# Projecting the values by rows of tokens, stored to memory and loaded in two token orders, in a hybrid decoder layer

## The chip, the cores and the metric

The kernel runs on one core of one Trainium2 chip. The metric is the device time of one execution in microseconds (us). A core has five engines with instruction queues of their own: PE (matrix products; PEld is its weight load, which overlaps with products), DVE, ACT and POOL (elementwise work), and SP, which here issues the DMA transfers between memory (DRAM) and the on-chip buffer. Products land in PSUM, eight banks of 128 x 512 fp32.

## The reference

One decoder layer on 1024 tokens of width 1024, in fp32. The mixer has a pooling branch (256 channels) and twelve rotary attention heads of width 64, each evaluated three times, with keys at stride 1, 4 and 16. The change concerns the values v.

```python
h = rms_norm(x, ln_pre_mix[l])
proj = h @ w_in[l]
u_pool = proj[..., :POOL_WIDTH]
q = proj[..., POOL_WIDTH:POOL_WIDTH + ATTN_WIDTH].reshape(B, S, N_HEADS, HEAD_DIM)
k = proj[..., POOL_WIDTH + ATTN_WIDTH:POOL_WIDTH + 2 * ATTN_WIDTH].reshape(B, S, N_HEADS, HEAD_DIM)
v = proj[..., POOL_WIDTH + 2 * ATTN_WIDTH:].reshape(B, S, N_HEADS, HEAD_DIM)
q, k = rope(q, pos), rope(k, pos)
pool_out = multi_scale_pool(u_pool, w_pool[l], pool_scale[l])
attn_out = dilated_attention(q, k, v).reshape(B, S, ATTN_WIDTH)
mix = jnp.concatenate([pool_out, attn_out], axis=-1) @ w_out[l]
x = x + rms_norm(mix, ln_post_mix[l])
h = rms_norm(x, ln_pre_ffn[l])
f = (jax.nn.silu(h @ w_gate[l]) * (h @ w_up[l])) @ w_down[l]
x = x + rms_norm(f, ln_post_ffn[l])
```

## The kernel before

**Numbers.** Every fp32 operand of a product is split into a high and a low part of a faster type: ACT casts the high part (L151 for weights), DVE or POOL subtracts it for the low part (L155). A product is three matmuls, high-high, high-low and low-high. `wtile` loads a weight tile of 512 KB into one of two raw buffers (`wraw`) and splits it into one of two split buffers (`whl`).

**Attention.** The heads make six pairs and the tokens two halves: twelve units, pairs 0 to 3 one after the other with both halves, then pair 4 half 0, pair 5 half 0, pair 4 half 1, pair 5 half 1 (`pa` and `pb` are pairs 4 and 5). A unit has scores (`ps_s`, L114), exponentials on ACT (L535), a merge and weighing of the three evaluations (`weigh`, on POOL L586 and DVE), transposes of the weights (`ps_t<-pmt,pp` and `ps_t<-idt,pp`, L117; split into `ptr` by ACT L626 and DVE L627), and products with the values (`ps_o<-ptr,v`). Its result goes to memory (`mixd`) and comes back for the output projection (`mraw`, `m`, L863 to L869).

**Order.** PE's instructions keep the order in which the program emits them. A table of positions, counted in units (`PRM`, put into a plan and sorted), sets that order. Beside the steps of units it holds `Fill` objects: projections cut into single steps, drawn in threes at even distances through a unit, and one at a time by `pull` between matmuls whose operand is strided. The other engines' instructions are put in order by a scheduler, as buffers come free; each engine runs its own list strictly in order. Buffers come from named pools: PSUM tags pj, s, o and t have two banks each.

**Values.** `v_half` is a `proj_half` for one pair: weights stationary, 512 tokens moving, 24 matmuls into one pj bank; `v_done` (L447) scales by the token norm on DVE into `vT`, channels by tokens. `v_turn` then turns `vT` by PE transposes into the two token orders that the products want: `nat` 1, tokens with stride 4, each transpose preceded by a pulled fill matmul, and `nat` 0, contiguous. Four transposes fill a ps_t bank; ACT (L480) casts it and DVE (L481) subtracts. That is 288 matmuls and 96 transposes in all. Unit 0's fill is pair 0's values up to position 0.33, then the pooling projection (`pool_proj`, `ps_pj<-whl,x`, two token tiles of 256 columns in a bank, evicted by ACT at L697). The fills of the units 2, 4, 6, 7, 8, 9 and 10 hold the other values.

## Time and profile before

| | |
|---|---|
| runs (three) | 1203.65, 1204.16, 1205.82 us, median 1204.16 |
| profiled execution | 1204.66 us, span 1202.8 us, mean granted clock of PE 0.982 |
| attention | until about 490 us of the span |
| most executed PE group in it | 720 matmuls of 512 columns, `ps_pj<-x,whl`, 215.3 us busy |

The profile is read from the top: the share that each engine is busy, the chain of work that ended last, then single groups of instructions, with their busy time, mean duration in ns, and the idle time ahead of them with its releaser. Matmuls overlap, so a matmul of 419 ns mean duration does not take 419 ns of PE's stream; start times of neighbours give the pitch. A row of the timeline has start, length, engine, line, operation, names, and in brackets the idle time ahead and what ended it.

Two more rows help to place the transposes of values, 96 in PE's list, and what follows them.

```profile
L117 PE MATMUL ps_t<-idt,vT 128*128 128x128 f32 x96 | 20.0, 280 | 4.4 <-DVE ptr L627 4.0 <-DVE v L481 0.3
L117 PE MATMUL ps_t<-pmt,pp 128*128 128x128 f32 x180 | 28.7, 281 | 4.0 <-DVE v L481 3.9
```

### The profile page before, as it was taken

Reading aid. Unit: us, or ns where it says so; the run is one execution under the profiler, and the core shown is the slowest. Engines: PE = TensorE matmul, PEld = TensorE weight load, DVE = VectorE, ACT = ScalarE, POOL = GpSimd, SP = SyncE. Lnnn points to the kernel's source line nnn. Section 1 sums busy time; section 2 is a strip of 40 time slices with the busy share of each in tenths; the row PEclk is TensorE's granted clock in tenths of the full one; section 3 lists DMA queues with packets and bytes.
Section 4 is the critical chain, followed back from the end, with each engine's and each line's share of the span. In section 5 each row is a group of like instructions: output and inputs, shape, how many; then the busy total and the mean of one; then the engine's idle time right before and its main releaser. Section 6 shows DMA issues by size and latency. Waiting matters only on the chain.

```text
span 1202.8 us, 16715 instructions
## 1 busy us (share of the span) xinstructions
PE 1156.9 (96%) x5942; PEld 982.1 (82%) x5942; DVE 793.6 (66%) x1467; ACT 541.1 (45%) x1021; POOL 595.6 (50%) x537
## 2 busy tenths in 40 slices
PE   8999999999999799999999999999999999999996
PEld 6898988878888687878888888888888888888896
DVE  7947877676778656678865756566665465454585
ACT  7456655554546565475522232232322335443430
POOL 0141625354245222242276776577764977656521
PEclk9999999999999899989999999999999999999998
DMA  7111101011011312562044444455434759765642
GB/s 271 56 40 36 45 27 45 27 45 45 27 44 46 95 71 88 199 238 97 18 149 184 157 170 154 167 195 190 147 129 173 277 183 391 240 210 193 193 140 71
DMA packets 68435, 158.60 MB, mean 132 GB/s; under 512 B 8064, under 2 KB 11392, under 8 KB 66944
## 3 DMA queue, kind: packets, MB, share of 16 engines
q1 hardware_dynamic: 67776, 157.01, 37.2%
q8 instruction: 47, 0.77, 0.3%
q10 hardware_dynamic: 576, 0.52, 0.1%
q14 instruction: 36, 0.29, 0.1%
HBM read 114.51 MB, written 42.99 MB: 131 GB/s over the span
## 4 chain that ended last, share of the span: by engine, by line
PE 81%; DVE 10%; issue 3%; ACT 3%; DMA 2%; POOL 1%; SPq 0%; DVEq 0%; ACTq 0%; POOLq 0%
PE ps_pj L114 29%; PE ps_o L114 22%; PE ps_s L114 20%; PE ps_t L114 7%; PE ps_t L117 3%; DVE pp L532 1%; DVE whl L155 1%; DVE ptr L627 1%; DMA wraw<-in_w_out_dram 1%; DVE sq L999 1%; DMA mraw<-mixd 1%; DMA xraw<-in_xT_dram 0%; DVE k L340 0%; DVE rsw L315 0%; DVE v L481 0%
## 5 line engine op out<-in xcount | busy, mean ns | idle before, releaser
L114 PE MATMUL ps_pj<-x,whl 128*128 128x512 f32 x720 | 215.3, 419 | 1.5 <-ACT whl L151 0.9
L114 PEld LDWEIGHTS ps_pj<-x,whl 128*128 128x128 f32 x720 | 131.0, 192 | 19.0 <-ACT whl L151 1.1
L1218 POOL TENSOR_TENSOR fw<-rw,fw 128x512 fp32r<-128x512 f32 x74 | 101.8, 1401 | 65.4 <-ACT fw L1216 65.4
L586 POOL TENSOR_SCALAR pp<-pp,wv 128x256 f32<-128x256 f32 (+1 forms) x156 | 72.6, 485 | 106.2 <-DVE wv L570 100.2
L114 PE MATMUL ps_o<-tT,fw 128*128 128x512 f32 x504 | 117.8, 390 | 0.0
L535 ACT ACTIVATE pp<-pp,sx 128x128 f32<-128x128 f32 (+1 forms) x192 | 89.5, 468 | 48.2 <-DVE sx L532 47.7
L114 PEld LDWEIGHTS ps_o<-tT,fw 128*128 128x128 f32 x504 | 94.7, 188 | 20.0
L1218 POOL TENSOR_TENSOR whl<-rw,whl 128x512 fp32r<-128x512 f32 x42 | 63.4, 1533 | 59.5 <-ACT whl L1216 59.5
L1216 ACT ACTIVATE fw<-rw 128x1024 fp32r<-128x1024 f32 x37 | 38.5, 1057 | 97.6 <-DMA rw<-in_w_up_dram 29.4
L1360 POOL TENSOR_TENSOR op<-rw,op 128x512 fp32r<-128x512 f32 x38 | 60.0, 1580 | 38.2 <-ACT op L1359 37.6
L317 POOL TENSOR_TENSOR rsw<-rsw,sinr 128x512 f32<-128x512 f32 x20 | 26.2, 1308 | 105.3 <-DVE rsw L315 105.3
L1359 ACT ACTIVATE op<-rw 128x1024 fp32r<-128x1024 f32 x38 | 40.3, 1061 | 67.2 <-PE ps_t L114 26.7
L626 ACT ACTIVATE ptr<-ps_t 128x512 fp32r<-128x512 f32 (+1 forms) x84 | 48.3, 576 | 47.9 <-PE ps_t L117 43.1
L627 DVE TENSOR_TENSOR ptr<-ps_t,ptr 128x512 fp32r<-128x512 f32 (+1 forms) x84 | 55.9, 668 | 17.2 <-ACT ptr L626 16.3
L114 PE MATMUL ps_o<-ptr,v 128*128 128x128 f32 (+1 forms) x472 | 59.5, 262 | 4.6 <-DVE ptr L627 4.4
L155 POOL TENSOR_TENSOR whl<-wraw,whl 128x512 fp32r<-128x512 f32 x34 | 45.9, 1371 | 34.6 <-ACT whl L151 33.8
L114 PE MATMUL ps_pj<-b,fw 128*128 128x512 f32 x264 | 62.3, 392 | 0.0
L114 PEld LDWEIGHTS ps_o<-ptr,v 128*128 128x128 f32 x472 | 53.4, 168 | 8.3 <-DVE ptr L627 4.8
L114 PEld LDWEIGHTS ps_pj<-b,fw 128*128 128x128 f32 x264 | 49.6, 188 | 10.9
L114 PE MATMUL ps_s<-k,qh 128*128 128x128 f32 (+1 forms) x192 | 53.1, 287 | 3.4 <-DVE sx L532 3.4
L114 PEld LDWEIGHTS ps_s<-k,qh 128*128 128x128 f32 x192 | 48.3, 252 | 7.4 <-DVE sx L532 3.7
L114 PE MATMUL ps_o<-tT,whl 128*128 128x512 f32 x216 | 52.3, 397 | 0.0
(303 smaller groups left out, 2888.9 us busy)
## 6 DMA issues: line engine op xcount, KB each, us to landing
rw<-bd SPq DMA_DIRECT2D x77, 256.0 KB, 4.6
rw<-wsd SPq DMA_DIRECT2D x44, 256.0 KB, 4.0
rw<-in_w_gate_dram SPq DMA_DIRECT2D x20, 512.0 KB, 3.5
rw<-in_w_up_dram SPq DMA_DIRECT2D x20, 512.0 KB, 4.6
wraw<-in_w_in_dram SPq DMA_DIRECT2D x17, 512.0 KB, 3.5
bd<-p SPq DMA_DIRECT2D x33, 256.0 KB, 2.5
rw<-in_w_down_dram SPq DMA_DIRECT2D x33, 256.0 KB, 5.0
fw<-in_w_down_dram SPq DMA_DIRECT2D x16, 512.0 KB, 4.1
```

The source lines that it names most:

```text
L114: return tc.keep_in_program_order(nc.tensor.matmul(*a, **k))
L117: return tc.keep_in_program_order(nc.tensor.transpose(dst, src, by))
L155: eng.tensor_tensor(dst[:, 1, at:at + w], src[:, at:at + w], dst[:, 0, at:at + w].bitcast(F32), ALU.subtract)
L317: eng[0].tensor_tensor(s, s, sinr[:, sl], ALU.mult)
L535: nc.scalar.activation(pt[:, j, lo:], pt[:, j, lo:], AF.Exp, bias=sx[:, 0, side, j, hd, 0:1], scale=-1.0, accum_out=sx[:, 0, side, j, hd, ...
L586: nc.gpsimd.tensor_scalar(pv, pv, un.wv[:, side, j, hd:hd + 1], 1.0, op0=ALU.mult, op1=ALU.mult)
L626: nc.scalar.activation(ptr[:, 0, :w], t[:, :w], AF.Copy)
L627: nc.vector.tensor_tensor(ptr[:, 1, :w], t[:, :w], ptr[:, 0, :w].bitcast(F32), ALU.subtract)
L1216: nc.scalar.activation(w[n][:, :, 0], raw[n], AF.Copy)
L1218: low[0] = nc.gpsimd.tensor_tensor(w[n][:, i, 1], raw[n][:, i], w[n][:, i, 0].bitcast(F32), ALU.subtract)
L1359: nc.scalar.activation(w[:, :, 0], raw, AF.Copy)
L1360: nc.gpsimd.tensor_tensor(w[:, 0, 1], raw[:, 0], w[:, 0, 0].bitcast(F32), ALU.subtract)
```

## The change

Values of two pairs (256 columns of the weights) are projected at once, with 128 tokens stationary and the weights moving, so that they come out with tokens in the partitions. The weights are laid out anew on the host as a further input, `w_v`, in two tiles per two pairs (the two halves of the summed dimension, `kh`). `v_rows(n, h)` does half h of the tokens for pairs 2n and 2n + 1: 96 matmuls of 256 columns, in steps of two, over two pj banks of two token tiles each; the order is first half of the sum for both banks, then second half for both. ACT evicts a tile with the token norm as scale into `vs` (one buffer, shared with the rotary product of k), and SP stores two tiles to the DRAM tensor `vd`. `v_load` loads a half of a pair in both token orders into `vr` (one buffer), ACT casts and POOL subtracts. In all 576 matmuls of 256 columns, 12 stores and 24 loads of 256 KB, no transposes of values. Each call of `v_rows` but the two of unit 0 loads its own two weight tiles, ten in all where there were six. Unit 0 now projects the values of pairs 0 and 1, up to position 0.5; units 2, 4, 6 and 9 the rest; unit 10 has no fill left.

```diff
-        'vt': ((1.12, 1.16, 1.3, 1.58), (3.0, 3.1, 3.3, 3.58), (5.0, 5.1, 5.3, 5.58), (7.0, 7.1, 7.3, 7.58),
-               (8.95, 9.05, 9.2, 9.45), (10.08, 10.16, 10.36, 10.46)),
-        'pw': 0.33,
+        'vt': ((0.9, 1.06, 1.1, 1.16, 1.3, 1.45), (2.8, 3.0, 3.05, 3.1, 3.3, 3.45), (4.8, 5.0, 5.05, 5.1, 5.3, 5.45),
+               (6.8, 7.0, 7.05, 7.1, 7.3, 7.45), (8.8, 8.95, 9.0, 9.8, 9.88, 9.95), (9.98, 10.08, 10.12, 10.2, 10.36, 10.42)),
+        'pw': 0.5,
...
+    vd = dram.tile([NPAIR // 2, T, 2 * P], F32, name="vd")
...
-    def v_done(pr, h, ps):
...
-    def v_half(pr, h):
-        return proj_half(3 * pr.p + 2, h, pr.st, lambda ps: v_done(pr, h, ps))
...
+    def v_rows(n, h, box=None):
+        box = {} if box is None else box
+        def product(t, kh, k, i):
+            if (kh, k, i) == (0, 0, 0) and t % 2 == 0:
+                if "w" not in box:
+                    box["w"] = [wv0 if n + kk == 0 else wtile(w_v[n][kk]) for kk in range(2)]
+                box["ps", t // 2] = bank("pj")
+            ps = box["ps", t // 2][:, t % 2 * 256:t % 2 * 256 + 256]
+            a, b = PASSES[i]
+            at = h * 512 + t * P
+            mm(ps, xk[4 * kh + k][:, b, at:at + P], box["w"][kh][:, a, k * 256:k * 256 + 256],
+               start=(kh + k + i + t % 2 == 0), stop=(kh == 1 and k == 3 and i == 2), skip_group_check=True)
+            if (kh, k, i) == (1, 3, 2):
+                if t % 2 == 0:
+                    box["to"] = qkp.tile([P, 2, 256], F32, name="vs", tag="rcl", bufs=1)
+                nc.scalar.activation(box["to"][:, t % 2], ps, AF.Copy, scale=norm["r"][:, 4 * h + t:4 * h + t + 1])
+                if t % 2:
+                    did(("vd", n, h))
+                    nc.sync.dma_start(vd[n, at - P:at + P].rearrange("(j p) f -> p j f", p=P), box["to"])
+        jobs = [(t, kh, k, i) for t2, kh in ((0, 0), (2, 0), (0, 1), (2, 1)) for t in (t2, t2 + 1)
+                for k in range(4) for i in range(3)]
...
+        return [lambda x=jobs[i:i + 2]: two(x) for i in range(0, len(jobs), 2)]
...
-        def step(nat, h):
+        def load(h):
+            need(("vd", pr.p // 2, h), 2)
+            box[h] = qkp.tile([P, 2, 4, P], F32, name="vr", tag="vT", bufs=1)
+            src = vd[pr.p // 2, h * 512:h * 512 + 512, pr.p % 2 * P:pr.p % 2 * P + P]
+            nc.sync.dma_start(box[h][:, 1], src.rearrange("(r c) f -> r c f", c=4))
+            nc.sync.dma_start(box[h][:, 0], src.rearrange("(j r) f -> r j f", j=4))
+        def cut(nat, h):
             dst = pr.v[nat, h] = room(nat, h)
...
-            for j in range(4):
-                if nat:
-                    pull()
...
-                turned_to(t[:, j * P:(j + 1) * P], src, idt)
...
-            nc.scalar.activation(hi, tv, AF.Copy)
-            nc.vector.tensor_tensor(dst[:, :, :, 1], tv, hi.bitcast(F32), ALU.subtract)
...
+            nc.scalar.activation(hi, raw, AF.Copy)
+            nc.gpsimd.tensor_tensor(dst[:, :, :, 1], raw, hi.bitcast(F32), ALU.subtract)
...
-        fill[2 * p] += [q_half(pr, 1), v_half(pr, 0), v_half(pr, 1)]
+        fill[2 * p] += [q_half(pr, 1), v_rows(*((1, 0), (1, 1), (2, 0))[p - 1])]
...
-    fill[7] += [q_half(pa, 0), k_half(pa, 1), v_half(pa, 0)]
-    fill[8] += [v_half(pa, 1), k_half(pb, 0), q_half(pb, 0), k_half(pb, 1)]
-    fill[9] += [q_half(pa, 1), q_half(pb, 1), v_half(pb, 0)]
-    fill[10] += [v_half(pb, 1)]
+    fill[7] += [q_half(pa, 0), k_half(pa, 1), k_half(pb, 0)]
+    fill[8] += [q_half(pb, 0), k_half(pb, 1), q_half(pa, 1)]
+    fill[9] += [v_rows(2, 1), q_half(pb, 1)]
...
```

The positions of pool weights, pooling means and of unit 0's scores move by a few hundredths, and the flags that choose DVE for a split (`we`) are renumbered; two splits of value weights move from DVE to POOL. Row lines of the changed kernel are its own: L153 and L157 are the old L151 and L155, L319 and L322 the old L317 and L320, L603 the old L586, L886 the old L869.

Three places in the order follow; the numbers in names tell buffers apart. First PE in unit 0, where the values' projection comes to its second half of the sum. Before (the first value weights, in a buffer of k, `k_279`, stationary, 512 tokens moving, into one bank):

```order
L114 MATMUL ps_pj_353<-x6_119,k_279 128x512 x3
L117 MATMUL ps_o_398<-idt_265,n1r_376 128x128 x4
L114 MATMUL ps_pj_353<-x7_120,k_279 128x512 x3
L114 MATMUL ps_pj_422<-x0_113,k_279 128x512 x3
L117 MATMUL ps_o_426<-idt_265,n1r_376 128x128 x4
L114 MATMUL ps_pj_422<-x1_114,k_279 128x512 x3
L114 MATMUL ps_pj_422<-x2_115,k_279 128x512 x3
L114 MATMUL ps_pj_422<-x3_116,k_279 128x512 x3
```

Now (tokens `x4` to `x7` stationary, weights `whl_356` moving):

```order
L114 MATMUL ps_pj_360<-whl_356,x6_120 128x256 x3
L114 MATMUL ps_pj_360<-whl_356,x7_121 128x256 x3
L114 MATMUL ps_pj_360<-whl_356,x4_118 128x256 x3
L114 MATMUL ps_pj_360<-whl_356,x5_119 128x256 x3
L114 MATMUL ps_pj_360<-whl_356,x6_120 128x256 x3
L114 MATMUL ps_pj_360<-whl_356,x7_121 128x256 x3
L117 MATMUL ps_o_470<-idt_266,n1r_382 128x128 x4
L114 MATMUL ps_pj_397<-whl_356,x4_118 128x256 x3
L114 MATMUL ps_pj_397<-whl_356,x5_119 128x256 x3
L114 MATMUL ps_pj_397<-whl_356,x6_120 128x256 x3
L114 MATMUL ps_pj_397<-whl_356,x7_121 128x256 x3
L114 MATMUL ps_pj_397<-whl_356,x4_118 128x256 x3
```

Bank 360 takes its first token tile up to the first row of x7, the second tile from the second row of x4 on, and bank 397 the same; between the two tiles of a bank nothing stands here, in later units sometimes products or four transposes. Before, a bank was one stretch of 24 matmuls with one reader at its end.

Second, PE in unit 9, where pair 4's query projection ends. Before, `whl_3840` is followed by a tile that was split earlier, `whl_3659`:

```order
L114 MATMUL ps_pj_3844<-x6_119,whl_3840 128x512 x2
L114 MATMUL ps_pj_3844<-x7_120,whl_3840 128x512 x2
L114 MATMUL ps_s_3911<-k_3645,qh_3741 128x128
L114 MATMUL ps_s_3911<-k_3645,ql1_91 128x128
L114 MATMUL ps_s_3911<-k_3645,qh_3741 128x256
L114 MATMUL ps_s_3911<-k_3645,ql1_91 128x256
L114 MATMUL ps_pj_3844<-x7_120,whl_3840 128x512
L114 MATMUL ps_pj_3934<-x0_113,whl_3659 128x512 x3
```

Now `whl_4022` is followed by the values' first tile `whl_4112`, which takes the same buffer; the other holds pair 5's query weights `whl_3740` until later:

```order
L117 MATMUL ps_t_4073<-idt_266,pp_3752 128x128 x4
L114 MATMUL ps_pj_4026<-x5_119,whl_4022 128x512 x2
L114 MATMUL ps_pj_4026<-x6_120,whl_4022 128x512 x3
L114 MATMUL ps_pj_4026<-x7_121,whl_4022 128x512 x3
L114 MATMUL ps_pj_4122<-whl_4112,x0_114 128x256 x3
L114 MATMUL ps_pj_4122<-whl_4112,x1_115 128x256 x3
L117 MATMUL ps_t_4134<-pmt_295,pp_3799 128x128 x4
L114 MATMUL ps_pj_4122<-whl_4112,x2_116 128x256 x3
L114 MATMUL ps_pj_4122<-whl_4112,x3_117 128x256 x3
```

The query projection of pair 5, which followed pair 4's, now follows the values; and the values' second tile, `whl_4118`, takes the buffer after `whl_4112`.

Third, POOL from unit 9's weighing on (pp). Before, the list ends with the subtractions of mix, `m00` and `m01`, then output weights and unit 10's weighing:

```order
L586 TENSOR_SCALAR pp_3906<-pp_3906,wv_4098 128x128
L586 TENSOR_SCALAR pp_3906<-pp_3906,wv_4098 128x256 x3
L586 TENSOR_SCALAR pp_3966<-pp_3966,wv_4098 128x128 x3
L586 TENSOR_SCALAR pp_4011<-pp_4011,wv_4098 128x128
L586 TENSOR_SCALAR pp_4011<-pp_4011,wv_4098 128x256 x3
L869 TENSOR_TENSOR m00_4293<-mraw_4238,m00_4293 128x512 x2
L869 TENSOR_TENSOR m01_4317<-mraw_4238,m01_4317 128x512 x2
L155 TENSOR_TENSOR whl_4352<-wraw_4350,whl_4352 128x512 x2
L586 TENSOR_SCALAR pp_4185<-pp_4185,wv_4454 128x256 x2
L586 TENSOR_SCALAR pp_4259<-pp_4259,wv_4454 128x256 x4
```

Now the rotary product (rsw, rco), output weights (whl_4618) and the cuts of values stand behind them. `v1_4451` and `v0_4460` are pair 4's second half, `v1_4515` and `v0_4532` pair 5's first half, whose loads into the one buffer `vr` come after the cuts of pair 4's:

```order
L603 TENSOR_SCALAR pp_4282<-pp_4282,wv_4377 128x128
L603 TENSOR_SCALAR pp_4282<-pp_4282,wv_4377 128x256 x3
L886 TENSOR_TENSOR m00_4564<-mraw_4519,m00_4564 128x512 x2
L886 TENSOR_TENSOR m01_4588<-mraw_4519,m01_4588 128x512 x2
L319 TENSOR_TENSOR rsw_4467<-rsw_4467,sinr_269 128x512
L157 TENSOR_TENSOR whl_4618<-wraw_4616,whl_4618 128x512 x2
L498 TENSOR_TENSOR v1_4451<-vr_4422,v1_4451 128x8x64
L498 TENSOR_TENSOR v0_4460<-vr_4422,v0_4460 128x8x64
L322 TENSOR_TENSOR rco_4468<-rco_4468,rsw_4467 128x512
L498 TENSOR_TENSOR v1_4515<-vr_4480,v1_4515 128x8x64
L498 TENSOR_TENSOR v0_4532<-vr_4480,v0_4532 128x8x64
L498 TENSOR_TENSOR vlast_4609<-vr_4552,vlast_4609 128x8x64 x2
```

The cuts of values, which DVE made out of PSUM, have joined POOL's list behind seven older pieces of work.

More of the change, by code (lines that the diff above doesn't have):

```diff
@@ L439, in done, with two, v_load @@
             rope(ps, h, pr.k, True, eng("rk", pr.p, h))
-        return proj_half(3 * pr.p + 1, h, pr.st, done)
-    def v_done(pr, h, ps):
-        if h == 0:
-            pr.vT = qkp.tile([P, T], F32, name="vT", tag="vT", bufs=1)
-        sl = slice(h * 512, (h + 1) * 512)
-        did(("vT", pr.p, h))
-        nc.vector.tensor_tensor(pr.vT[:, sl], ps, rb[:, sl], ALU.mult)
-    def v_half(pr, h):
-        return proj_half(3 * pr.p + 2, h, pr.st, lambda ps: v_done(pr, h, ps))
-    def v_turn(pr):
-        pr.v = {}
+        return proj_half(2 * pr.p + 1, h, pr.st, done)
+    def v_rows(n, h, box=None):
[19 more added lines that the diff above has]
+                for k in range(4) for i in range(3)]
+        def two(x):
+            for y in x:
+                product(*y)
+        return [lambda x=jobs[i:i + 2]: two(x) for i in range(0, len(jobs), 2)]
+    def v_load(pr):
+        pr.v, box = {}, {}
         def room(nat, h):
@@ L637, in product @@
             need(("t", pr.p), 2 if h == 0 else 4)
-            await_(("ptr", pr.p, h, hd, gi))
+            await_(("ptr", pr.p, h, hd, gi), ("v", pr.p, h))
             clock[0] += 0.7
@@ L825, in hybrid_block @@
     for p, at in enumerate(G["vt"]):
-        st = later(v_turn, pairs[p])
-        put([lambda i=i, st=st: st(i) for i in range(2)], at[0], at[1])
-        put([lambda i=i, st=st: st(i) for i in range(2, 4)], at[2], at[3])
+        st = later(v_load, pairs[p])
+        for i, x in enumerate(at):
+            put([lambda i=i, st=st: st(i)], x, 0)
     fill = [[] for u in range(12)]
```

37 lines of the change are left out of this document (16 added, 21 removed), and 4 rows, old and new, of the table PRM.

## The prediction

> **What bounds the kernel now.** I read the page's busy shares first, then the chain that ended last, then the waits of the tensor engine (total us, times, longest).
>
> ```profile
> PE 1156.9 (96%) x5942; PEld 982.1 (82%) x5942; DVE 793.6 (66%) x1467; ACT 541.1 (45%) x1021; POOL 595.6 (50%) x537
> PE 81%; DVE 10%; issue 3%; ACT 3%; DMA 2%; POOL 1%; SPq 0%; DVEq 0%; ACTq 0%; POOLq 0%
> ```
>
> ```profile
> PE ps_o L114 <- DVE ex L550: 5.1, 5, 1.4
> PE ps_o L114 <- DVE ptr L627: 4.9, 3, 2.6
> PE ps_t L117 <- DVE v L481: 4.2, 4, 2.5
> PE ps_t L117 <- DVE ptr L627: 4.0, 1, 4.0
> PE ps_s L114 <- DVE sx L532: 3.4, 3, 2.0
> PE ps_pj L114 <- ACT uf L697: 2.4, 4, 0.7
> PE ps_t L117 <- POOL pp L586: 1.2, 1, 1.2
> ```
>
> PE works 96% of the span, so the sum is kept on PE: what leaves its stream is gained in full, and every wait that enters it is lost in full. Work on the other engines counts only through such waits. I reckon against the profiled execution, 1204.66 us (span 1202.8), which is 0.5 us above the median of the runs, 1204.16.
>
> **Removed: the 96 transposes of values.** Start times of single rows give their pitch.
>
> ```profile
> 392.05 0.27 PE L117 MATMUL ps_t<-idt,vT 128*128 128x128 f32 x1
> 392.40 0.27 PE L117 MATMUL ps_t<-idt,vT 128*128 128x128 f32 x1
> 394.11 1.80 PE L114 MATMUL ps_pj<-x,whl 128*128 128x512 f32 x7
> 412.60 0.60 PE L117 MATMUL ps_t<-idt,vT 128*128 128x128 f32 x4
> 412.95 0.37 PE L114 MATMUL ps_s<-k,qh 128*128 128x256 f32 x1
> ```
>
> A strided transpose and the projection matmul drawn behind it take 392.40 - 392.05 = 0.35 us. Seven such matmuls alone end in 1.80, one lasts about 0.40, so their pitch is 1.40/6 = 0.233 and the transpose costs 0.117. Four contiguous ones take 0.35, 0.088 each. 48 x 0.117 + 48 x 0.088 = **-9.8 us**. With them go the waits that the transposes cause or stand in: 4.2 (next user of the bank after the value subtraction) and 4.0 (a value transpose held until the bank is read), **-8.2**.
>
> **The projection in halves.** 288 matmuls of 512 columns become 576 of 256.
>
> ```profile
> 45.35 3.04 PE L114 MATMUL ps_pj<-whl,x 128*128 128x256 f32 x24
> 54.94 0.33 PE L114 MATMUL ps_s<-k,qh 128*128 128x128 f32 x1
> 55.28 0.34 PE L114 MATMUL ps_s<-k,ql 128*128 128x128 f32 x1
> ```
>
> 24 of them (pooling projection) take 3.04 with 0.30 for the last, pitch 2.74/23 = 0.119. 576 x 0.119 - 288 x 0.233 = **+1.5**. Between strided scores a step now draws two halves. A score with one half takes 0.34, no less than with a whole one, so a second half comes on top: 0.12. In the new order 19 scores are followed by exactly two halves, before it was one: 18 x 0.12 = **+2.2** (0, if the weight load hides it, to 46 pulls x 0.12 = 5.5).
>
> **Added: evictions that PE waits for.** A bank now holds two token tiles. The second tile's last twelve matmuls wait until ACT has evicted the first. The pooling projection does this already.
>
> ```profile
> 48.49 0.47 ACT L697 ACTIVATE uf<-ps_pj,n1r 128x256 f32<-128x256 f32 x1 [0.23 <-PE ps_pj L114]
> 49.01 6.09 PE L114 MATMUL ps_pj<-whl,x 128*128 128x256 f32 x46 [0.62 <-ACT uf L697]
> mixd<-mix SPq DMA_DIRECT2D x14, 256.0 KB, 2.0
> bd<-p SPq DMA_DIRECT2D x33, 256.0 KB, 2.5
> mraw<-mixd SPq DMA_DIRECT2D x6, 512.0 KB, 4.7
> ```
>
> Twelve banks, twelve waits. Six are this one: 0.62 each in unit 0 (two), about 0.45 in units 2, 4, 6, 9, where transposes sometimes lie between: 3.0. In the other six ACT's eviction must also wait for the staging tile, which has one buffer and is still being stored: 0.47 + 0.1, a store of 2.0 to 2.5 (no row shows these stores; the first two DMA rows, stores of as many bytes, are the bounds), 0.47 + 0.1 = 3.1 to 3.6. PE has twelve halves meanwhile (1.43): 1.9 lost, twice in unit 0; elsewhere eight or so small products and transposes more (0.9): 1.0, four times. Together 3.0 + 3.8 + 4.0 = **+10.8**. Low end 4.4, if only unit 0's stand (2 x 0.62 + 2 x 1.6); high end 15.6, if two ACT copies of about 0.6 stand ahead of the eviction in those four units. Behind the waiting ACT stand exponentials and copies of transposed weights, for which PE waits next.
>
> **Added: the weight tile of unit 9.** Two split-weight tiles exist, and pair 5's query weights now occupy one until the values of pairs 4 and 5 are done. Pair 4's query weights and both value tiles then use the other in turn, each behind its cast and subtraction.
>
> ```profile
> L151 ACT ACTIVATE whl<-wraw 128x1024 fp32r<-128x1024 f32 x33 | 34.8, 1056 | 15.1 <-PE ps_pj L114 10.6 <-PE ps_s L114 4.0 <-PE ps_t L114 0.3
> L155 POOL TENSOR_TENSOR whl<-wraw,whl 128x512 fp32r<-128x512 f32 x34 | 45.9, 1371 | 34.6 <-ACT whl L151 33.8 <-POOL fw L155 0.8
> L317 POOL TENSOR_TENSOR rsw<-rsw,sinr 128x512 f32<-128x512 f32 x20 | 26.2, 1308 | 105.3 <-DVE rsw L315 105.3
> L315 DVE STREAM_SHUFFLE rsw<-ps_pj 128x512 f32<-128x512 f32 x20 | 14.8, 742 | 0.1
> L535 ACT ACTIVATE pp<-pp,sx 128x256 f32<-128x256 f32 x132 | 65.8, 500 | 28.2 <-DVE sx L532 28.0
> ```
>
> First value tile: the POOL queue has the rotary product ahead: 0.74 + 1.31 + 1.37 = 3.4, less two halves 0.24: 3.2. Second half of it: 0.3. Second tile: 1.06 + 1.37 less two halves and a score: 2.1. **+5.6**; bounds 2.1 (only the casts show) and 7.6 (an exponential of 0.5 ahead of each cast, twice).
>
> **Added: the last loads of values.** This is the largest term. Pair 5's first half is loaded into a one-buffer tile after pair 4's second half has been cut out of it, and POOL cuts (DVE did before). The order puts everything in one POOL queue behind unit 9's weighing.
>
> ```profile
> 384.00 6.54 POOL L586 TENSOR_SCALAR pp<-pp,wv 128x128 f32<-128x128 f32 x13 [0.63 <-DVE wv L570]
> 395.22 4.98 POOL L869 TENSOR_TENSOR m<-mraw,m 128x512 fp32r<-128x512 f32 x4 [4.68 <-ACT m L867]
> L480 ACT ACTIVATE v<-ps_t 128x512 fp32r<-128x512 f32 x22 | 12.7, 583 | 7.3 <-PE ps_t L117 7.3
> 398.42 0.82 PE L117 MATMUL ps_t<-pmt,pp 128*128 128x128 f32 x3 [2.51 <-DVE v L481]
> 399.88 1.37 PE L114 MATMUL ps_o<-ptr,v 128*128 128x128 f32 x8
> 407.76 1.13 PE L117 MATMUL ps_t<-idt,vT 128*128 128x128 f32 x4 [4.02 <-DVE ptr L627]
> ```
>
> From the start of the weighing: 6.5 weighing, 5.0 for four mix subtractions, 1.3 rotary, 2.7 output weights, 2.7 two cuts, then load 2.5 (no row shows it; 2.0 to 2.5 by the stores of 256 KB, 4.7 by the loads of mix, which have twice the bytes; I take the nearest in size), cast 0.6, cut 1.4: 22.8 us until PE has values for pair 5's products. PE has 11 transposes (1.0), 9 matmuls of 512 (2.1), 4 products (0.5) and 16 scores (1.9, at the pitch of 256 columns) in that time and starts 0.5 later: 6.0. **+16**, in place of the 2.51 and 4.02 already taken out. Today those products start 15.9 after the weighing does, with far more PE work ahead of them. Low end 1.4, if POOL's queue is no limit and only the way through memory counts (0.6 eviction, store 2.0, load 2.0, 0.6, two cuts 2.7, load 2.0, 0.6, 1.4 = 11.9 against 10.5 of PE); high end 20, with loads of 4.7 and POOL slowed.
>
> **The clock.** Time slices of 4 us, with PE's busy time first and the granted clock behind POOL's count; in the first PE waits 2.00 of 4 us, in the third 2.64.
>
> ```profile
> 194.00:198.00 4.00, 2.00 (x10) 1.52 (x9) 3.91 (x12) 1.76 (x8) 3.92 (x4) 0.89 0.00 0
> 198.00:202.00 4.00, 4.00 (x19) 3.49 (x18) 3.89 (x10) 3.25 (x9) 0.61 (x1) 0.69 0.39 133
> 264.00:268.00 4.00, 1.36 (x10) 1.12 (x10) 3.73 (x12) 2.71 (x10) 0.00 (x0) 1.00 0.45 131
> 268.00:272.00 4.00, 4.00 (x26) 3.41 (x25) 2.04 (x4) 0.93 (x2) 0.00 (x0) 1.00 0.00 0
> 408.00:412.00 4.00, 4.00 (x14) 3.52 (x14) 1.61 (x3) 1.22 (x3) 0.00 (x0) 0.50 0.09 34
> ```
>
> After the first wait 4.0 us of work ran at 0.69 and 2.0 at 0.89: 1.4 us lost; after the second none. So about half of the waits near 2 us cost 1.4 more. Two to four such are new: **+2** (0 to 5). After the tail's waits the clock is at 0.50 already today; I leave that.
> The Trainium skill, "TensorE: Matmul & The Clock Gate", section "HAM oscillation — how this bites in real kernels", sets the harmful gap at more than about 3.4 us. By that rule the new waits of 2 us lose no clock and the time is 2 us lower, 1220.8. The row at 198 differs from the rule, a gap of 2.00 us was enough, so I keep the row.
>
> **Relief of DVE.**
>
> ```profile
> L481 DVE TENSOR_TENSOR v<-ps_t,v 128x512 fp32r<-128x512 f32 x22 | 15.1, 686 | 8.7 <-ACT v L480 8.7
> L447 DVE TENSOR_TENSOR vT<-ps_pj,rb 128x512 f32<-128x512 f32 x12 | 8.2, 686 | 0.8 <-PE ps_pj L114 0.6
> ```
>
> It loses 22 subtractions of 0.69 and 12 scalings of 0.69, 15.1 + 8.2 = 23.3 us of 793.6; PE waits 5.1 + 4.9 + 3.4 = 13.4 us for its ex, ptr and sx. Until 490 us, where attention ends, it is busy some 490 x 0.7 = 340, so a fifteenth goes; a fifteenth of 13.4 would be 1. Queues shorten by more than the mean, so I take **-2** (0 to -6, nearly half). Other engines: ACT evicts 24 tiles (0.47) for the copies it made anyway; POOL gets 24 cuts of 1.37, 33 us, and four more weight tiles, covered by its 50% idle time except where named. 12 stores and 24 loads of 256 KB and four of 512 KB add 11 MB to 158.
>
> **Sum.** -9.8 - 8.2 + 1.5 + 2.2 + 10.8 + 5.6 + 16 + 2 - 2 = +18.1, so 1204.66 + 18.1 = **1222.8 us**. All low ends give -14.6 (1190), all high ends +37 (1242).
>
> **Rivals.**
> *The tail is light.* POOL idles 4.68 us ahead of its mix subtractions today; if the cuts found such room, the tail would cost 5 rather than 16: 1211.8. Against it: in the new order the rotary product and output weights stand in that room.
> *Faster: the waits are covered.* The stall of one place gives the other engines a lead for the next. Then evictions cost 4.4, unit 9 2.1, the tail 1.4 and DVE's relief is 6: 1190 to 1200, say 1197. For it: PE's waits today are short. It decides if the store lands within PE's work and the last load is off POOL's queue.
> *Nothing.* New waits of 14 us instead of 32 give the gains back exactly: 1204.7.
> *POOL becomes the bound.* If a cut of 1.37 stands ahead of the weighing in each of ten units, transposes of weights come later by that: 13.7 more, 1236.5. For it: PE waited 1.2 for POOL's weighing once already. Against: in most units the cuts stand behind it.
> That the transposes stay is excluded: the order has none left.
>
> **Chances and range.** Forecast 0.50, light tail 0.20, faster 0.13, nothing 0.06, POOL 0.11. Faster by over 0.2% (2.4 us, about what can be told from no change): 0.13; same 0.06; slower 0.81. From 1200 to 1235 the range leaves out most of the faster case, half of POOL's and the forecast's edges, some 0.19.
>
> **What would show it.** In the changed profile PE's waits should list the value eviction on ACT some twelve times, 8 to 13 us in all; the subtraction on POOL of pair 5's values near 16 us in one wait; whl on ACT and POOL near 6 us in the ninth unit. No PE row should read idt,vT. If the largest wait is under 6 us, the tail's step is wrong; if the evictions sum to under 5, the store was hidden; if weighing on POOL leads the waits, the last rival holds.

## The result and the profile after

The changed kernel takes 1235.27 us, median of four runs (1234.60 to 1237.29), against 1204.31 for the kernel before in the same session (1203.65 to 1205.82). The ratio is 1.026, with an interval of 1.024 to 1.028: slower by 31 us. The forecast of 1222.8 had the direction, but the time lies 0.3 us beyond the end of the range.

The page of the changed kernel, busy times and the chain that ended last (the execution that was profiled took 1234.6 us, span 1232.7):

```profile
PE 1156.8 (94%) x6134; PEld 987.2 (80%) x6134; DVE 780.1 (63%) x1429; ACT 555.4 (45%) x1049; POOL 640.6 (52%) x573
PE 75%; DVE 9%; issue 5%; ACT 5%; DMA 4%; POOL 2%; SPq 0%; ACTq 0%; POOLq 0%; DVEq 0%
```

Two things stand in the first line. PE's idle time, span less busy, was 1202.8 - 1156.9 = 45.9 us and is 1232.7 - 1156.8 = 75.9: 30.0 more, which is all of the difference of the spans (29.9). And PE's busy time has not fallen, although the transposes are gone. Both need a cause.

The waits of PE in the changed kernel (total us, times, longest):

```profile
PE ps_s L114 <- DVE sx L549: 14.0, 6, 11.0
PE ps_pj L114 <- ACT vs L459: 11.7, 10, 2.4
PE ps_o L114 <- POOL v L498: 10.0, 1, 10.0
PE ps_pj L114 <- POOL whl L157: 6.2, 3, 3.9
PE ps_o L114 <- DVE ptr L644: 5.3, 6, 1.7
PE ps_pj L114 <- ACT whl L153: 2.4, 2, 1.3
PE ps_o L114 <- DVE ex L567: 1.5, 1, 1.5
PE ps_t L117 <- POOL pp L603: 0.7, 2, 0.5
```

The rows for `ps_t<-idt,vT` and for the value subtraction on DVE are gone. The value eviction on ACT is there, ten times. The weight tile of unit 9 is there: 6.2 + 2.4 = 8.6, of which 1.5 stood under the same names before. The tail, forecast as one wait of 16, is two waits of 11.0 and 10.0 with a small one of 1.4 ahead. The larger of them has DVE as its releaser, which the forecast did not have at all.

The timeline of the changed kernel at that place, PE first (start, length, engine, line, operation, names, idle time ahead and its releaser):

```profile
427.36 0.58 PE L114 MATMUL ps_s<-k,qh 128*128 128x256 f32 x1 [11.02 <-DVE sx L549]
438.58 1.54 PE L114 MATMUL ps_o<-ptr,v 128*128 128x128 f32 x8 [10.01 <-POOL v L498]
```

DVE, POOL, ACT and SP's queue in the same stretch:

```profile
415.10 11.51 DVE L886 TENSOR_TENSOR m<-mraw,m 128x512 fp32r<-128x512 f32 x2
426.54 0.41 DVE L549 CUSTOM_DVE_ANT_0 pp<-ps_s,mB 128x256 f32<-128x256 f32 x1
429.31 1.22 DVE L157 TENSOR_TENSOR xk<-wraw,xk 128x1024 fp32r<-128x1024 f32 x1
...
413.18 4.97 POOL L886 TENSOR_TENSOR m<-mraw,m 128x512 fp32r<-128x512 f32 x4
418.10 1.26 POOL L319 TENSOR_TENSOR rsw<-rsw,sinr 128x512 f32<-128x512 f32 x1
419.32 2.48 POOL L157 TENSOR_TENSOR whl<-wraw,whl 128x512 fp32r<-128x512 f32 x2
421.76 2.48 POOL L498 TENSOR_TENSOR v<-vr,v 128x512 fp32r<-128x512 f32 x2
424.20 1.26 POOL L322 TENSOR_TENSOR rco<-rco,rsw 128x512 f32<-128x512 f32 x1
437.26 2.70 POOL L498 TENSOR_TENSOR v<-vr,v 128x512 fp32r<-128x512 f32 x2 [11.80 <-ACT v L497]
...
430.55 0.81 SPq L149 DMA_DIRECT2D wraw<-in_w_out_dram  x2
431.53 0.53 SPq L489 DMA_DIRECT2D vr<-vd  x1
...
436.55 0.63 ACT L497 ACTIVATE v<-vr 128x512 fp32r<-128x512 f32 x1 [4.81 <-DMA vr<-vd]
```

Two mix subtractions on DVE, 0.7 us each elsewhere, last 11.51 us: the first of them alone takes 10.91, the second 0.68. POOL runs ten two-operand instructions without a gap from 413.18 to 424.20 + 1.26 = 425.46, and the first subtraction ends 0.6 us after that, at 426.0. Behind those two stand the exponents' sums (`sx`), for which PE's scores wait: the 11.0. That is a reading so far; the experiments test it.

The second wait continues from there. Pair 4's last cuts end at 424.2, and `vr` is free. But SP issues the load of `vr` at 431.5, behind the loads of a weight tile whose raw buffer DVE frees only at 429.31 + 1.22 = 430.53. The first half of the load, which PE needs first, is issued at 431.53, and ACT begins to cast it at 436.55, 5.0 us later; then come a cast of 0.63 and the first cut of about 1.3: PE goes on at 438.58, 10.0 late.

The clock, in windows of the kernel before and then of the changed one (length, then busy time of PE, PEld, DVE, ACT and POOL with counts, the granted clock, DMA share, GB/s):

```profile
340.00:440.00 100.00, 88.82 (x510) 77.27 (x510) 71.10 (x188) 54.91 (x137) 45.74 (x61) 0.95 0.18 58
```

```profile
340.00:440.00 100.00, 66.42 (x409) 59.43 (x408) 62.68 (x155) 49.48 (x127) 48.57 (x56) 0.81 0.22 72
400.00:440.00 40.00, 16.30 (x95) 14.01 (x95) 27.43 (x45) 17.21 (x37) 22.69 (x27) 0.70 0.39 125
```

The stretch with the new waits ran at 0.81 instead of 0.95. That does not explain the busy time, for a low clock costs only while PE works, and in 400 to 440 PE worked 16.30 of 40.00 us. The traces record the granted clock as stretches of 1.00 and of 0.50. In a series of 512-column matmuls the start times are 0.23 us apart at 1.00 and 0.43 at 0.50 (medians, in both kernels). Added up over all stretches at 0.50, PE was busy in them for 31.1 us in the kernel before and for 31.6 in the changed one. The longest new one, 416.2 to 443.5, holds 6.3 us of work in 27.3; and between 110 and 325 us, where the kernel before has three such stretches, the changed one has none. So each kernel loses about 14 us of busy time to the clock (an estimate: 31 x (0.43 - 0.23) / 0.43), and the difference between them is 0.2. The forecast's 6.1 us of removed work (-9.8 + 1.5 + 2.2) did not go to the clock; it came out as about -0.3.

### The profile page after: what moved, and what is told of

Its sections match the earlier page's. It is cut to its first block, busy times and chain, and to the rows that moved or that the text cites. A ratio compares the mean times of both kernels' runs of the same rounds, so it can differ in the third digit from the quotient of the medians.

```text
span 1232.7 us, 17214 instructions
## 1 busy us (share of the span) xinstructions
PE 1156.8 (94%) x6134; PEld 987.2 (80%) x6134; DVE 780.1 (63%) x1429; ACT 555.4 (45%) x1049; POOL 640.6 (52%) x573
## 4 chain that ended last, share of the span: by engine, by line
PE 75%; DVE 9%; issue 5%; ACT 5%; DMA 4%; POOL 2%; SPq 0%; ACTq 0%; POOLq 0%; DVEq 0%
PE ps_pj L114 26%; PE ps_o L114 21%; PE ps_s L114 19%; PE ps_t L114 6%; PE ps_t L117 2%; DMA vr<-vd 1%; ACT pp L552 1%; DVE pp L549 1%; DMA mraw<-mixd 1%; DVE m L886 1%; POOL pp L603 1%; DVE k L342 1%; DVE ptr L644 1%; DVE whl L157 1%; POOL whl L157 1%
## 5 line engine op out<-in xcount | busy, mean ns | idle before, releaser
L114 PE MATMUL ps_pj<-x,whl 128*128 128x512 f32 x480 | 144.2, 415 | 1.7 <-POOL whl L157 1.6
L114 PE MATMUL ps_pj<-whl,x 128*128 128x256 f32 x672 | 106.2, 299 | 21.6 <-ACT vs L459 11.7
L114 PEld LDWEIGHTS ps_pj<-whl,x 128*128 128x128 f32 x672 | 91.4, 198 | 26.2 <-ACT vs L459 14.5
L157 POOL TENSOR_TENSOR whl<-wraw,whl 128x512 fp32r<-128x512 f32 x46 | 61.6, 1358 | 92.3 <-ACT whl L153 52.9
L603 POOL TENSOR_SCALAR pp<-pp,wv 128x256 f32<-128x256 f32 (+1 forms) x156 | 71.7, 478 | 61.3 <-DVE wv L587 61.3
L114 PEld LDWEIGHTS ps_pj<-x,whl 128*128 128x128 f32 x480 | 86.5, 193 | 12.6 <-POOL whl L157 2.0
L1376 ACT ACTIVATE op<-rw 128x1024 fp32r<-128x1024 f32 x38 | 40.2, 1060 | 67.2 <-PE ps_t L114 30.7
L114 PEld LDWEIGHTS ps_s<-k,qh 128*128 128x128 f32 x192 | 48.6, 253 | 18.8 <-DVE sx L549 16.5
L114 PEld LDWEIGHTS ps_pj<-b,fw 128*128 128x128 f32 x264 | 49.6, 188 | 10.9
```

What stands on the lines that cost most here:

```text
L114: return tc.keep_in_program_order(nc.tensor.matmul(*a, **k))
L157: eng.tensor_tensor(dst[:, 1, at:at + w], src[:, at:at + w], dst[:, 0, at:at + w].bitcast(F32), ALU.subtract)
L603: nc.gpsimd.tensor_scalar(pv, pv, un.wv[:, side, j, hd:hd + 1], 1.0, op0=ALU.mult, op1=ALU.mult)
L1376: nc.scalar.activation(w[:, :, 0], raw, AF.Copy)
```

## The experiments

Four theories were open for the 31 us: the evictions (store and bank), the weight tile of unit 9, POOL's queue in the tail, and DVE standing still beside POOL. The first seven runs each undo one of them in the changed kernel, or move it; the others combine edits. None leaves out work. The kernel before took 1205.2 to 1205.6 us in these sessions. Ratios are to it, with their interval.

### Two staging tiles

```diff
-    box["to"] = qkp.tile([P, 2, 256], F32, name="vs", tag="rcl", bufs=1)
+    box["to"] = qkp.tile([P, 2, 256], F32, name="vs", tag=("rcl", "rsw")[t // 2], bufs=1)
```

> The changed kernel with one difference: the two banks of a value projection are staged for the store in two different buffers (the second one shares the buffer of the rotated columns, rsw), so an eviction never waits for the store before it. Store theory: of the ten waits of PE on ACT's value eviction (11.7 us in the changed kernel) the second-bank ones (2.40, 1.86, 1.26, 1.26, 1.40, 1.06) fall to 0.3 to 0.7 each, the sum to 5 to 6 us, the time from 1235 to about 1229. Rival, the bank alone makes the wait (a bank being read is not written, whatever the store does): the sum stays over 10 us and the time within 2 us of 1235.

Measured: 1228.54 us, ratio 1.019 (1.016 to 1.022). The waits on the eviction, in the run with two tiles:

```profile
PE ps_pj L114 <- ACT vs L459: 7.7, 10, 1.3
```

From 11.7 to 7.7. The two second waits of unit 0 fell from 2.40 and 1.86 to 0.56 and 0.61, and the one of unit 6 from 1.40 to 0.56, so there the store was the cause, as forecast. In units 2 and 4 the waits of 1.26 stayed with a second tile: the store was not what PE waited for there. In the trace of unit 2 ACT makes three copies of 0.6 in a row, from 172.11 on, ahead of the eviction at 173.74. The forecast had the size (1.0) by the wrong cause; it had named copies on ACT for its high end only.

The run also shows what a wait does to the clock. The stretch behind the wait of 1.86, in the changed kernel (with the one behind the wait of 2.40 first) and then with two tiles:

```profile
48.00:52.00 4.00, 3.82 (x32) 3.82 (x33) 3.91 (x8) 2.74 (x6) 0.00 (x0) 1.00 0.02 4
...
60.00:64.00 4.00, 2.14 (x17) 1.93 (x17) 0.00 (x0) 0.47 (x1) 0.00 (x0) 1.00 0.49 150
64.00:68.00 4.00, 4.00 (x21) 4.00 (x21) 2.16 (x9) 3.04 (x11) 0.00 (x0) 0.58 0.18 61
```

```profile
64.00:68.00 4.00, 3.63 (x29) 3.22 (x27) 2.65 (x12) 3.33 (x14) 0.00 (x0) 1.00 0.59 173
```

After the wait PE worked 4.00 us at 0.58, some 1.7 us lost on top of the 1.86; without it the clock stayed at 1.00. Behind the wait of 2.40 in the same unit it stayed at 1.00 too. Which wait costs the clock changes from run to run: six traces have both waits, and a stretch at 0.50 of 3.4 us or more begins within 2 us of the 1.86 in five of them and of the 2.40 in two; each has at least one. The runs in which these waits are 0.9 or less have none there. The Trainium skill, "TensorE: Matmul & The Clock Gate", section "HAM oscillation — how this bites in real kernels", sets the harmful gap at more than about 3.4 us; these rows disagree, for a wait of 1.86 was enough.

### The two banks in turn

The order of a row of projections goes over both banks alternately, so that twelve or more matmuls of the other bank stand between an eviction and the next use of its bank; two staging tiles as well.

```diff
+    box["to", t // 2] = qkp.tile([P, 2, 256], F32, name="vs", tag=("rcl", "rsw")[t // 2], bufs=1)
...
-    jobs = [(t, kh, k, i) for t2, kh in ((0, 0), (2, 0), (0, 1), (2, 1)) for t in (t2, t2 + 1)
+    jobs = [(t, kh, k, i) for t, kh in ((0, 0), (1, 0), (2, 0), (3, 0), (0, 1), (2, 1), (1, 1), (3, 1))
```

> Two staging buffers as in the run before, and in the second half of the sum the tiles come in the order first of bank 1, first of bank 2, second of bank 1, second of bank 2, so twelve matmuls of the other bank lie under each eviction. Store and bank theories together: PE's waits on the value eviction fall under 2 us in all, the time to about 1224 (11.7 less). Rival, the waits are only moved (ACT or the store queue is late anyway and PE waits for something else in the same places): the sum falls but the time stays over 1230.

Measured: 1217.71 us, ratio 1.010 (1.008 to 1.012), 17.6 less than the changed kernel. The evictions are down to one wait of 0.9. The gain is larger than the 11.7 of waits; the page says where the rest is:

```profile
PE 1149.6 (95%) x6134; PEld 982.4 (81%) x6134; DVE 777.8 (64%) x1429; ACT 555.7 (46%) x1049; POOL 642.3 (53%) x573
```

Span 1214.6, so idle time fell by 75.9 - 65.0 = 10.9, and busy time by 7.2 for the same 6134 matmuls. At a clock of 0.50 PE is now busy for 18.8 us instead of 31.6, which is worth about 6 of the 7.2. The two tail waits stood as before (11.7 and 9.8).

### A third weight tile in unit 9

```diff
-                if h == 0 or mt == 8:
+                if h == 0 or mt in (8, 10):
```

Pair 5's query weights are loaded again for its second half and do not occupy a split tile through unit 9.

> The changed kernel, but pair 5's query weights are loaded and split a second time for its second half (as pair 4's are), so that they do not occupy a split tile while unit 9 projects values. Tile theory: PE's waits on whl in unit 9 (1.15, 3.93, 1.30, 0.72 = 7.1 us) fall under 2.5 us, the time falls by 4 to 6 us to about 1230. Rival, POOL is late in unit 9 anyway (a cut and a rotary product stand ahead of the weight subtraction): the first wait, 5 us, stays, and the time falls by 2 us or less.

Measured: 1224.44 us, ratio 1.016 (1.014 to 1.018), 10.8 less. Both `whl` rows are gone from PE's waits. Again idle time fell by less, 75.9 - (1222.0 - 1152.6) = 6.5, and busy time by 4.2; PE's work at 0.50 fell from 31.6 to 24.6 us, worth about 3 of it.

### Pair 5's values first

In the table of positions pair 5's first half is loaded and cut before pair 4's second.

```diff
-    (8.8, 8.95, 9.0, 9.8, 9.88, 9.95), (9.98, 10.08, 10.12, 10.2, 10.36, 10.42)),
+    (8.8, 8.95, 9.0, 10.04, 10.08, 10.1), (9.02, 10.01, 10.02, 10.2, 10.36, 10.42)),
```

> The changed kernel, but the values of pair 5, first half, are loaded right after the cuts of pair 4, first half, and cut first in the tail; pair 4's second half is loaded after them. Chain theory (load behind cuts behind one buffer): PE's wait of 10.0 us on POOL's cut falls under 2 us, the wait of 11.0 us on DVE (sx) stays, the time falls by 8 to 11 us to about 1226. Rival, POOL's queue alone is late: the cut that PE waits for comes only one or two places earlier in it (2.5 us), so the wait stays over 6 us.

Measured: 1235.8 us, ratio 1.025 (1.022 to 1.027): no gain. The wait on POOL's cut fell from 10.0 to 4.5, and the one on DVE stayed (10.0). But the idle time is 1234.8 - 1158.9 = 75.9, the same to a tenth. What was saved in the tail was lost at other waits: at the norm on POOL behind attention (`nrr`, 2.2, new), at a copy of transposed weights on ACT (`ptr`, 1.7, new), at the sums of squares (4.7 instead of 3.2), and the rest in small ones. A miss for both theories (under 2, over 6): a wait was shortened, the end did not move.

### The mix subtractions all on POOL, and all on DVE

Two edits of one expression, in two runs. The theory that DVE stands still beside POOL says: give the two subtractions to POOL, and the next two-operand instruction of DVE stands still instead; give all to DVE, and POOL's chain loses four of its ten.

```diff
-                (nc.gpsimd if h == 0 and n < 2 else nc.vector).tensor_tensor(
+                (nc.gpsimd if h == 0 else nc.vector).tensor_tensor(
```

> The changed kernel with the three mix subtractions that DVE has in the tail (m03 twice, m02) given to POOL. In the changed kernel two of them take DVE 11.5 us (0.7 each alone) and end 1.2 us after POOL's unbroken chain of two-input subtractions. Theory of a shared path (a DVE subtraction of two operands from the on-chip buffer stands still while POOL works on such ones): DVE reads scores on at once, PE's wait of 11.0 us on sx falls under 3; POOL's chain grows by 2.5 to 3.7 us, so the load of pair 5's values and PE's wait for them (10.0) come out longer, 16 to 22; the time stays within 4 us of 1235. Rival, late data (the mix had not landed): the wait on sx stays near 11, now as a wait of POOL.

```diff
-                (nc.gpsimd if h == 0 and n < 2 else nc.vector).tensor_tensor(
+                (nc.vector).tensor_tensor(
```

> The changed kernel with all seven mix subtractions of the first half on DVE, so POOL's chain in the tail is four of them (5.0 us) shorter. Shared path: DVE's subtractions take 0.7 where POOL idles and wait where it has the rotary product, weights and cuts; the chain on POOL ends about 5 us earlier after the weighing, PE's two waits of the tail (11.0 + 10.0) sum to 14 to 17, the time falls by 4 to 7 us. Rival, DVE as the bound: seven subtractions on DVE's list delay the reading of scores, the two waits stay over 20 and the time does not fall.

All on POOL: 1235.2 us, ratio 1.027 (1.023 to 1.030). The 11 us wait for `sx` is gone, and the next one has grown by as much, as the theory expected. Late data, its rival, is out: POOL makes the moved subtractions without waiting, in the usual 1.27 each. PE's waits, then DVE and POOL on the timeline of this run:

```profile
PE ps_o L114 <- POOL v L498: 21.7, 1, 21.7
PE ps_s L114 <- DVE sx L549: 3.3, 5, 1.4
```

```profile
419.14 0.69 DVE L644 TENSOR_TENSOR ptr<-ps_t,ptr 128x512 fp32r<-128x512 f32 x1
420.43 12.24 DVE L157 TENSOR_TENSOR xk<-wraw,xk 128x1024 fp32r<-128x1024 f32 x1
...
415.61 6.21 POOL L886 TENSOR_TENSOR m<-mraw,m 128x512 fp32r<-128x512 f32 x5
430.32 1.27 POOL L322 TENSOR_TENSOR rco<-rco,rsw 128x512 f32<-128x512 f32 x1
```

This is the clearest reading of the study. POOL is busy from 415.61 to 431.59. DVE's subtraction at 419.14, which has one operand in PSUM (`ps_t`), takes its usual 0.69. The next, with both operands in the on-chip buffer, takes 12.24 where it takes 1.22 in the changed kernel, and ends 1.1 us after POOL's chain, so nearly all of its work can lie behind the chain. It is another instruction on other data than the one that stood still in the changed kernel. SP's load waits for it as before, and PE waits once for 21.7 instead of 11.0 and 10.0.

The Trainium skill, "SBUF — State Buffer", section "Who interferes with whom", says that a DVE instruction with two inputs in the buffer contends with a POOL instruction that reads the buffer, under an exclusive lock, and that one with at most one such input does not. The trace agrees with both: 12.24 us in the one case, 0.69 in the other. If the lock went with each instruction, the price would be at most one POOL instruction of 1.3 us (an estimate from the rows above); measured is the rest of the running one and eight more.

All on DVE: 1226.1 us, ratio 1.018 (1.015 to 1.022), 9.2 less than the changed kernel, more than the 4 to 7 expected. The longest wait for `sx` is 2.8 and the cut's is 8.6. DVE and POOL in this run:

```profile
415.11 2.43 DVE L886 TENSOR_TENSOR m<-mraw,m 128x512 fp32r<-128x512 f32 x2
...
415.26 3.40 POOL L157 TENSOR_TENSOR whl<-wraw,whl 128x512 fp32r<-128x512 f32 x2
418.63 3.51 POOL L498 TENSOR_TENSOR v<-vr,v 128x512 fp32r<-128x512 f32 x2
```

Here both engines get through side by side: DVE takes 2.43 for two (1.4 alone), POOL 3.40 and 3.51 for two (2.48 in the changed kernel). So a collision costs either DVE the rest of the chain, or each engine about 1 us over two instructions. A third way stands in the changed kernel itself, 10 us ahead of the standstill:

```profile
404.43 2.53 POOL L157 TENSOR_TENSOR whl<-wraw,whl 128x512 fp32r<-128x512 f32 x2 [15.87 <-ACT whl L153]
404.50 1.27 DVE L583 TENSOR_TENSOR de<-dd,sx 128x32 f32<-128x32 f32 x1 [1.22 <-ACT dd L581]
405.80 1.19 DVE L584 TENSOR_TENSOR nm<-de 128x16 f32<-128x16 f32 x1
```

Two small DVE instructions, 0.2 us each elsewhere (medians 0.19 and 0.18), lasted as long as one POOL instruction each, and the first got through between the two. What decides between these was not found.

### The cuts on DVE

```diff
-            nc.gpsimd.tensor_tensor(dst[:, :, :, 1], raw, hi.bitcast(F32), ALU.subtract)
+            nc.vector.tensor_tensor(dst[:, :, :, 1], raw, hi.bitcast(F32), ALU.subtract)
```

> The changed kernel with the 24 cuts of values on DVE, as before the change (there from PSUM, here from the on-chip buffer). POOL queue theory of the forecast: the tail's chain on POOL is 2.7 us shorter ahead of the load and 1.4 behind it, and the first wait in unit 9 on whl (3.93) falls by 1.3; the time falls by 4 to 6 us. Shared path: POOL's chain ahead of the standstill's end is 2.5 shorter, but each cut on DVE can itself stand still behind POOL, so DVE's cuts take well over 0.7 in the mean and the time falls by 0 to 4. Rival, relief lost: DVE gets 24 x 0.7 = 17 us back, waits of PE on ex, ptr and sx grow, and the time rises.

Measured: 1230.74 us, ratio 1.022 (1.019 to 1.024), 4.5 less. The wait for the cut is 5.1, the one for `sx` still 9.1: without the cuts POOL's chain is shorter by 2.5, and DVE's stop with it (9.59 us for the two mix subtractions, before 11.51). The time alone does not tell the theories apart; the stop that shrank with the chain does. The cuts on DVE hardly stood still (median 0.69, two of 24 longer), against the expectation.

The run also tests the relief of DVE. DVE has its work back (794.4 us busy, 793.6 in the kernel before), and yet PE's waits for its `ex`, `ptr` and `sx` outside the tail are 1.5 + 5.0 + 3.1 = 9.6, against 8.4 in the changed kernel and 13.4 before. So DVE's load accounts for some 1.2 of the 5.0 us that these waits lost; what took the rest away is not shown.

### Together

> Banks in turn with two staging buffers, and pair 5's query weights loaded twice (the edits of two earlier runs together: those took 17.6 and 10.9 us off the changed kernel's 1235.3). If both are places of their own, the time is 1235.3 - 28.5 = 1206.8, within 3. If they share a cause (the lead that one wait gives to other engines fills the next), it is 1211 to 1217. The tail's two waits should still be there, 20 us in all; that they are still there while the time is near that of the kernel before (1205) would show that all other parts of the change gain about as much as the tail loses.

Banks in turn and third tile: 1216.7, ratio 1.010 (1.008 to 1.013), where the single gains added to 1206.8. The waits of both kinds are gone, but PE has a new one:

```profile
PE ps_o L117 <- POOL nrr L182: 4.8, 1, 4.8
```

At 552 us, after attention, POOL's norm (`nrr`) stands behind two splits of the following weights (`fw`, 3.48 us), as in the run with pair 5's values first; in the other runs the scheduler put `nrr` first. That explains 4.8 of the 10 that are missing. Most of the others are busy time: the third tile alone took 4.2 off it, here it is 2.2 above that of the banks alone, with 25.3 us of work at a clock of 0.50 instead of 18.8. The tail was as before, 11.7 and 9.8.

> Banks in turn with two staging buffers, and all mix subtractions of the first half on DVE. Two places with causes of their own: 1235.3 - 17.6 - 9.2 = 1208.5, within 3. If the tail's wait only moves when PE comes to it sooner, 1212 to 1218.

Banks in turn and the mix on DVE: 1210.76, ratio 1.004 (1.002 to 1.006), within the 3 us of two separate places.

> As the run before, with pair 5's query weights loaded twice as well. In the earlier pair of runs that edit brought 7 us of waits on whl but 4.8 us came back at the start of the feed-forward part, where POOL's list had a weight subtraction ahead of the norm's (nrr); here the list has nrr first. If that position was the reason, this is 5 to 7 us under the run before (about 1202); if the tile's gain is eaten by something else, within 2 us of it.

With the third tile as well: 1199.18 (1197.49 to 1200.92), ratio 0.995 (0.993 to 0.997). Beside these two edits the third tile brought 11.6, as much as alone (10.8) and more than the 5 to 7 expected. PE's largest wait is the cut on POOL, 8.8.

> As the run before, with the cuts of values on DVE too. POOL has then nothing new in the tail but the weight split, so the way from the last eviction to pair 5's values is two DMA transfers, casts and cuts: PE's wait for the values falls from about 8.6 to 5 or less, and the time to 1196 to 1202. If DVE's added 17 us bind, or its cuts stand still behind POOL, the time is that of the run before or more.

With the cuts on DVE too: 1199.96, ratio 0.996 (0.994 to 0.998), no gain. The wait for the cut is 8.2, on DVE instead of POOL, where 5 or less was expected. Most of it is the load through memory: issued at 395.93, it is cast at 399.89. The other 2.1 us are DVE's list, which comes to the cut at 401.95, behind the rotary casts.

> As the run before, with pair 5's first half loaded ahead of unit 9's projection and cut first. Then no load of the tail stands between PE and the values that it needs first: the wait on pair 5's values falls under 2 us and the time is 3 to 6 us under the run before, about 1195, which is 0.8% faster than the kernel before the change; rival, the earlier load run showed: the time saved there came back at the end of the attention, so within 2 us of the run before.

And with pair 5's values first: 1194.82 (1193.41 to 1196.39), ratio 0.992 (0.989 to 0.994). The edit that brought nothing by itself brings 5.1 here. The page and the wait for the cut in this run:

```profile
PE 1147.9 (96%) x6134; PEld 980.9 (82%) x6134; DVE 788.7 (66%) x1458; ACT 555.7 (47%) x1050; POOL 614.4 (51%) x545
```

```profile
PE ps_o L114 <- DVE v L498: 2.8, 1, 2.8
```

Span 1194.6, so PE idles 46.7 us, against 45.9 in the kernel before, and is busy 9.0 us less. With all five edits the change is faster than the kernel before by 0.8% (0.6 to 1.1). Most of that is clock: PE works for 16.1 us at 0.50, before for 31.1, worth about 7 of the 9.0. The mean granted clock is 0.988 in all four executions, and 0.981 to 0.985 in the thirteen of the kernel before in that session. PE's shorter work is left with about 2 us.

## Why the prediction was right and where it was wrong

Terms against the profile of the changed kernel, in us:

| term | forecast | measured | shown by |
|---|---|---|---|
| transposes, halves, pulls | -6.1 | about -0.3 | busy time 1156.9 and 1156.8, clock loss taken off |
| waits at transposes | -8.2 | -8.2 | both rows gone, but see below |
| evictions | +10.8 | +11.7 | one row; cut to 7.7 by one run, to 0.9 by another |
| weight tile of unit 9 | +5.6 | +7.1 | 8.6 less the 1.5 of before; removed by one run |
| tail | +16 | +22.4 | 11.0 + 10.0 + 1.4 |
| clock | +2 | about +0.2 | work at 0.50: 31.1 and 31.6 us |
| relief of DVE | -2 | -5.0, mostly not by DVE's load | 5.1 + 4.9 + 3.4 before; 1.5 + 5.3 + 1.6 outside the tail |

The measured waits give -8.2 + 11.7 + 7.1 + 22.4 - 5.0 = 28.0 of the 30.0 us of new idle time; 2 us are spread over small rows. The forecast had 22.2 for these and -4.1 for work and clock, where the profile has 30.0 and -0.1: 8 us missed in the waits and 4 in the work make the 12 us between 1222.8 and 1235. Two slips in the sum are small: 22.8 less 6.0 is 16.8 and not 16, and of 19 scores 18 were priced.

**The failed step is "Added: the last loads of values".** It laid the whole tail on the POOL queue, 22.8 us from the start of the weighing to the values, with PE's work subtracted. Measured from 407.87 to 438.58 it is 30.7. POOL's part was not the fault: weighing to last cut took 16.4 us where 18.2 were counted. Then the load was issued 7.3 us after that cut, where none was counted, and took 5.0 to the cast, where 2.5 was. POOL sat idle 11.8 us for ACT and the load. The step had DVE unaffected, even relieved. In the trace DVE stood still beside POOL's chain, which the change had lengthened by two cuts and pushed together with the output weights' split; PE lost 11.0 to that, and the same stop held back SP's queue, and so the load, for the second 10.0. The runs with the mix moved to POOL and to DVE show it: the wait moves with the instruction that collides, and it goes when four of POOL's ten are taken away. The step counted every instruction in POOL's queue, but not which of DVE's instructions cannot run beside them, and in SP's queue it had the load first when a weight load stood ahead of it.

The kernel before already showed such collisions:

```profile
399.38 1.91 DVE L155 TENSOR_TENSOR xk<-wraw,xk 128x1024 fp32r<-128x1024 f32 x1
402.93 3.63 DVE L869 TENSOR_TENSOR m<-mraw,m 128x512 fp32r<-128x512 f32 x3
402.45 2.96 POOL L155 TENSOR_TENSOR whl<-wraw,whl 128x512 fp32r<-128x512 f32 x2 [2.24 <-ACT whl L151]
```

The first row takes 1.22 in the changed kernel beside an idle POOL; here POOL's mix subtractions run until 400.20. The three subtractions of the second row would take 2.0. They stand ahead of the `ptr` for which PE waited 4.02. So this part of the -8.2 was a wait for DVE at the tail and not one that transposes cause, though its row went with them.

**The second step that failed is the removed work**, "Removed: the 96 transposes of values" with "The projection in halves". -6.1 was forecast and about -0.3 measured. Start-to-start times, added up by groups with the clock loss taken off, give -5.6 for transposes and projections together (forecast -8.3), about +2 for the scores between which the halves are drawn (as forecast), and +3 in groups that the change did not touch. Why those grew stays open. In the other runs the sum lies between +0.6 and -2.8.

**The clock** was forecast as +2 for new waits alone. It came out even. Between 110 and 325 us three stretches at 0.50 went, the first of them (from 197 us) right behind the wait of 2.00 for `sx` in the kernel before, and the slow stretch at the tail's waits holds little of PE's work. That a short wait can cost the clock was right: two experiments gave some 6 and 3 us of it back.

**Evictions and weight tile were right** in place and nearly in number and size: ten waits where twelve were forecast, 11.7 us for 10.8, and 7.1 us for 5.6. Within the evictions, units 2 and 4 waited for another cause than the store, and that their size fits is luck.

**Rivals.** The light tail and the faster case fell with the tail's 22 us. "POOL becomes the bound" named 1236.5, close to the time, but by another mechanism: transposes waiting for the weighing, and that row reads 0.7 us. The faster case needed the waits to be covered; only five further edits made them so.

## What to carry to other kernels

When elementwise work moves from operands in PSUM to operands in the on-chip buffer, look at what the other of DVE and POOL runs beside it: two-operand instructions of both collide, and a chain without gaps on POOL can hold DVE until its end. Price a new wait of PE with the clock behind it, by the work that runs in the slow stretch: taking 10.9 us of idle time out of dense work brought 17.6, while the tail's 21 us of waits lie in a stretch of 27.3 us at 0.50 that holds 6.3 us of work. Before a busy time is laid to the clock, add up PE's work at the low clock in both kernels. And a staging tile with one buffer puts the store's latency into the next product, and an in-order DMA queue puts the load of a tile behind any earlier load whose buffer is not free.

## What the runs showed of the hardware that was not expected

- A DVE instruction with two operands in the on-chip buffer lasted 10.91 us instead of 0.68, and another 12.24 instead of 1.22, beside an unbroken POOL chain; with one operand in PSUM it took its usual 0.69. In another run the two engines shared, 2.43 and 3.40 for two each. What decides is open.
- A wait of 1.86 us was followed by a granted clock of 0.50 for 3.4 us or more in five of six traces, one of 2.40 in two of them.
- Loads of 256 KB from `vd` took longer than stores of the same size, median 3.7 against 2.2 us from issue to landing:

```profile
vr<-vd SPq DMA_DIRECT2D x24, 256.0 KB, 3.7
vd<-vs SPq DMA_DIRECT2D x12, 256.0 KB, 2.2
```
